# A hybrid decoder trunk: recurrence units of four head pairs by two chunks in place of two head pairs by four chunks

## The chip, the cores and the metric

The kernel runs on one core of a Trainium2 chip. The time is device microseconds of that core for one execution of the whole program; it is a median over runs. All matmuls run on TensorE (PE), which executes its instructions in the order in which they stand. VectorE (DVE), ScalarE (ACT) and GpSimd (POOL) work beside it, and the sync engine (SP) issues every DMA of the program, also in order.

## The reference, cut to what matters

A trunk of two layers over 1024 tokens with model width 1024 and 16 heads of 64. Layer 0 mixes time with the RWKV-7 recurrence, layer 1 attends to one shared set of keys and values; each is followed by an MLP. The recurrence is the part that the change touches:

```
S_t = S_{t-1} diag(w_t) + (S_{t-1} a_t) b_t^T + v_t k_t^T ;  y_t = S_t r_t     (per head, S is 64x64)
y   = groupnorm(y) * ln_w + ln_b + bonus
out = (y * (sigmoid(xg @ g1) @ g2)) @ wo
```

The decay is `w_t = exp(-exp(w_log))`, and `w_log` comes from a small product with `w2`. All arrays are float32.

## The kernel before, in words

Two heads share the 128 partitions and are called a pair; there are 8 pairs, and tokens are cut into chunks of 64. Inside a chunk the recurrence is turned into products, so that only the state (64x64 a head) goes from chunk to chunk. The work is cut into 16 units (`phase_wkv`). Each holds 8 pair-chunks: 2 pairs by 4 chunks, that is 256 tokens. `where(u)` gives the half of the sequence, the first pair and the tokens of unit `u`.

A unit has four parts, each a generator that yields at places where other work may be put in:

- `early` loads the unit's vectors (`ar`, `bk`), makes the decays (the product with `w2`) and inverts 16x16 blocks.
- `late` builds the chunk matrices (`sc`, `tt`, `bkt`) from them and loads the values `uv`.
- `chain` is the serial part. For each chunk it makes on TensorE the state product `pq<-st,ar`, with the output product `py<-ar,st` of the same state; VectorE adds (`xs`); then comes the solve product `pq<-xs,tt`, which ScalarE and VectorE copy to `uv`; then the state update `pq<-uv,bkt`, which VectorE adds to the scaled old state (`st`); then the second output product `py<-sc,uv`. Each is two matmuls a pair, one for each head.
- `gate` normalizes the unit's outputs and multiplies them by the gate: for each pair it loads `g2` into a buffer of one copy and makes two products with it (`pms<-ga,g` and `pms<-zt,g`).

Beside the chain the kernel runs `early` two units ahead, `late` one ahead, `gate` one behind, and the dense projections and the MLP of the first half (`beside`). After each yield of `chain`, `step` takes so many yields of the others as the table of numbers says (`PR`, `NG`, `NA` and so on). Chain instructions are recorded at high priority, and a scheduler sets the final order on each engine. Dense matmuls are of 128x512 columns (tiles `pj` and `pk`, lines 124 to 128), three for each weight block, since each operand is split in a high and a low part. Their weights pass through a ring of two raw buffers (`wraw`), ScalarE and GpSimd.

The fp32 matmuls of the chain use only a part of the array: 64 rows by 64 columns for those on `st` and `xs`, 128 rows by 64 columns for those on `uv`. The rows of the trace write this part ahead of the shape of the moving operand (`64*64`, `128*64`).

Of the kernel before, what the change touches and what calls it, by code (L numbers as in the profile page):

```python
# [15 lines left out]
F32 = mybir.dt.float32  # L16
# [3 lines left out]
ALU = mybir.AluOpType  # L20
# [55 lines left out]
class K:  # L76
# [168 lines left out]
    def run(self, stop=99):  # L245
        tc, nc, ap = self.tc, self.nc, self.ap
        V, S = nc.vector, nc.scalar
        with ExitStack() as es:
# [90 lines left out]
            self.smalls = [(pg, "pms", 1), (px, "pmt", 1)]  # L339
            x[1] = self.load_x(self.pool(es, "x1"), 1)  # L340
            e3 = es.enter_context(ExitStack())
# [3 lines left out]
            with ExitStack() as e2:  # L345
                self.mod_pool = self.pool(e2, "mp"), 2, D
                hs = self.gated(1, hp1)
                self.take(m0, self.ND[0])
                self.drain(self.proj([hs], wo, range(KT), self.residual(x, self.G[:, 0:8]), lead=2))
                m1 = self.mlp(x, 0, (1,), hp1, md)  # L350
                self.take(m1, 2)
                self.take(m0, self.ND[1])
                self.drain(m0)
                self.take(m1, 40)

                def mods():
# [11 lines left out]
                rs = self.rs = [xq.tile([128, HT], F32, name=f"rs{j}") for j in range(2)]  # L368
# [31 lines left out]

    N0 = 17
    NR = 4
    NMD = 4.5
    SG = 2
    EF = 1
    NG8 = 0.8
    UA = 7
# [8 lines left out]
    NS = 1.5  # L416
    NA = 2.2
    NW = (2, 2)
    NB = 5.4
    NC = 3  # L420
    NP = (3, 3, 3)
    PR = 2.2
    NG = 2
    ND = (20, 40)
# [16 lines left out]
    def phase_rwkv(self, es):  # L441
# [73 lines left out]
        if self.RP:  # L515
            with tc.high_priority():
                self.take(r, 1)
            self.take(r, 16)
        else:
            self.take(r, 17)  # L520
        v = self.stream(h, 0, 0, xj, ev, al)
# [146 lines left out]
    def phase_wkv(self, es, rest, done):  # L668
# [5 lines left out]
        H = (slice(0, 64), slice(64, 128))  # L674
        C = 8
        W = C * HD

        def where(u):

            j, g, q = u // 8, u % 8 // 2, u % 2  # L680
            return j, 2 * g, slice(j * HT + q * 256, j * HT + (q + 1) * 256)

        two = lambda a: a.rearrange("p (q t) -> p q t", q=2)
        pair = lambda d, p, ts: d[p:p + 2, :, ts].rearrange("q p t -> p q t")
        wa, pool = self.pool(es, "wkva", 2), {}
# [4 lines left out]
        def erl(n, shape, bufs=2):  # L690
            return wa.tile(shape, F32, name=n, tag=n, bufs=bufs)
# [24 lines left out]
        def early(u, w):  # L716

            j, p, ts = where(u)
            w2 = erl("w2", [65, 2, 128], 1)
            nc.sync.dma_start(out=w2, in_=ap["w2"][p:p + 2].rearrange("q k n -> k q n"))  # L720
            ar = erl("ar", [128, 2, C, HD], 3)
            bk = erl("bk", [128, C, 2, HD])
            nc.sync.dma_start(out=two(ar[:, 0].rearrange("p c t -> p (c t)")), in_=pair(self.kkd, p, ts))
            for i, src in enumerate((self.bd, self.kpd)):
                for q in range(2):
                    nc.sync.dma_start(out=bk[:, q * 4:(q + 1) * 4, i], in_=src[p + q, :, ts].rearrange("p (c t) -> p c t", t=HD))
            nc.sync.dma_start(out=two(ar[:, 1].rearrange("p c t -> p (c t)")), in_=pair(self.Rd, p, ts))

            Pi = erl("sg", [128, W], self.SG)
            ps = bank("pe")  # L730
            for q in range(2):
                PE.matmul(out=ps[:, q * 256:(q + 1) * 256], lhsT=w2[:, q], rhs=self.zt[0:65, ts], start=True, stop=True)
            yield
# [14 lines left out]
            kr = erl("sg", [128, W], self.SG)  # L748
            for i in range(2):
                q = slice(i * 4, i * 4 + 4)  # L750
                V.scalar_tensor_tensor(out=c3(kr)[:, q], in0=bk[:, q, 1], scalar=self.col("rk", p + i), in1=ar[:, 1, q], op0=ALU.mult, op1=ALU.mult)
# [21 lines left out]
        def late(u, w):  # L773
# [11 lines left out]
            uv = lng("uv", [128, C, 2, HD])  # L785
            for q in range(2):
                nc.sync.dma_start(out=uv[64:128, q * 4:(q + 1) * 4], in_=self.Vd[ts, (p + q) * 128:(p + q + 1) * 128].rearrange("(c s) (e d) -> s c e d", s=64, d=HD))

# [57 lines left out]
        def chain(u, w):  # L846
# [3 lines left out]
            yp = bank("py")  # L850
            old = self.sv[:, p:p + 2]
            begin, end = ts.start == 0, ts.stop == T
            of = lambda a: a.rearrange("p (q c) d -> p q c d", q=2)
            pc, xk = pc.rearrange("p (q c) -> p q c", q=2), of(xk)
            us = [of(uv[0:64, :, e]) for e in range(2)]

            def small(n, bufs=2):
                return lng(n, [128, 2, HD], bufs)

            def scaled(st, c):  # L860
                sp = small("sp")
                G.tensor_tensor(out=sp, in0=st, in1=pc[:, :, c:c + 1].broadcast_to([128, 2, HD]), op=ALU.mult)
                return sp

            def state():
                return bank("pq")[:, 0:128].rearrange("p (q d) -> p q d", q=2)

# [7 lines left out]
            sp = None if begin else scaled(old, 0)  # L875
            for c in range(4):
                first, last = begin and c == 0, end and c == 3
                ys = [yp[:, (q * 4 + c) * HD:(q * 4 + c + 1) * HD] for q in range(2)]
                xs = xk[:, :, c]
                if not first:  # L880
                    ps = state()
                    for q in range(2):
                        ins = both(ps[:, q], ar[:, 0, q * 4 + c], st[:, q], True, True)
                    for q in range(2):
                        both(ys[q], st[:, q], ar[:, 1, q * 4 + c], c + q == 0, False)
# [5 lines left out]
                for q in range(2):  # L891
                    ins = both(ps[:, q], tt[:, q * 4 + c], xs[:, q], True, True)
                S.copy(out=us[0][:, :, c], in_=ps[H[0]])
                yield ins, V.tensor_copy(out=us[1][:, :, c], in_=ps[H[1]])
                ins2 = None
                if not last:
                    ps = state()
                    st = small("st", 3) if c < 3 else old
                    for q in range(2):
# [6 lines left out]
                    if c < 3:  # L906
                        sp = scaled(st, c + 1)
                for q in range(2):
# [8 lines left out]
        def gate(u, w):  # L917

            j, p, ts = where(u)
            y, bv, rs = w["y"], self.t(), self.t()  # L920
            ga = lng("ga", [128, 256], 1)
            nc.sync.dma_start(out=ga, in_=self.gad[:, ts])
# [7 lines left out]
            ps = self.small()  # L930
            for q in range(2):
                c = slice(q * 256, (q + 1) * 256)
                g2 = lng("g2", [128, 2, 128], 1)
# [531 lines left out]
```

## Time and profile before

| what | value |
|---|---|
| median of 3 runs | 3394.16 us (3393.62 to 3395.95) |
| the profiled execution's own time | 3400.13 us |
| its span, first to last instruction | 3398.3 us |
| mean granted TensorE clock | 0.967 of full speed |
| chain of recurrences, first to last | about 332 to 1306 us |

All durations below are of the one profiled execution; its own time is 5.97 us above the median of the runs. TensorE is the busiest engine by far. The recurrence's stretch is the part of the span in which its small matmuls and the dense ones share TensorE.

### The profile page before, as it was taken

To read this page: it belongs to the slowest core of one execution; us is meant where nothing else is said; L and a number is where in the kernel's file an instruction comes from. 1 tells how busy PE (TensorE), PEld (TensorE's weight loads), DVE (VectorE), ACT (ScalarE), POOL (GpSimd) and SP (SyncE) were. 2 spreads that over 40 slices of the span, in tenths; PEclk is the share of its full clock that TensorE was granted. 3 is DMA by queue.
4 is the path that set the end of the run, shared out by engine and by line. 5 is a ranking of instruction groups with operands and counts; after the bars stand their busy time and mean duration, and the time that the engine had idled before them with its cause. 6 is when DMAs were issued, how large, how long until landed. Compare 5 with 4: busy or idle time off the path is not lost. (4 is left out here: it accounts for less than half of the span.)

```text
span 3398.3 us, 50336 instructions
## 1 busy us (share of the span) xinstructions
PE 3219.0 (95%) x19108; PEld 2442.9 (72%) x19108; DVE 1947.4 (57%) x3239; ACT 1434.2 (42%) x2284; POOL 1367.2 (40%) x868
## 2 busy tenths in 40 slices
PE   4898999999999999899999999999999999999997
PEld 2456666666777777678887777777778888778886
DVE  7496765756556535366676433555576666454444
ACT  3642236533433223242233556667565554332223
POOL 3364432333333233454444432444433333554444
PEclk7898999999999999899999999999999999999999
DMA  7365344454333225335542233666644442232322
GB/s 276 97 233 154 94 126 135 125 144 148 91 99 105 82 76 186 118 127 176 175 161 87 85 131 119 202 207 179 175 134 137 143 134 100 87 112 93 99 97 83
DMA packets 294066, 452.90 MB, mean 133 GB/s; under 512 B 114721, under 2 KB 170433, under 8 KB 293825
## 3 DMA queue, kind: packets, MB, share of 16 engines
q1 hardware_dynamic: 293824, 449.68, 42.0%
q8 instruction: 152, 2.49, 0.3%
q14 instruction: 90, 0.73, 0.1%
HBM read 371.25 MB, written 78.32 MB: 132 GB/s over the span
## 5 line engine op out<-in xcount | busy, mean ns | idle before, releaser
L117 POOL TENSOR_TENSOR wl<-wraw,wh 128x1024 fp32r<-128x1024 f32 x385 | 953.1, 2477 | 1221.7 <-ACT wh L116 1139.6
L116 ACT CAST wh<-wraw 128x1024 fp32r<-128x1024 f32 x385 | 402.6, 1046 | 835.2 <-PE pk L126 358.0
L124 PE MATMUL pj<-hh,wh 128*128 128x512 f32 x1120 | 449.4, 409 | 7.7 <-DVE sq L1085 2.1
L128 PE MATMUL pj<-hh,wl 128*128 128x512 f32 x1120 | 444.7, 403 | 6.0 <-POOL wl L117 6.0
L126 PE MATMUL pj<-hl,wh 128*128 128x512 f32 x1120 | 443.1, 401 | 0.0
L1011 DVE SCALAR_TENSOR_TENSOR x<-pj,G,x 128x512 f32<-128x512 f32 x304 | 225.8, 747 | 167.4 <-PE pj L128 165.6
L128 PE MATMUL pk<-hh,wl 128*128 128x512 f32 x688 | 273.7, 404 | 11.2 <-POOL wl L117 11.2
L124 PE MATMUL pk<-hh,wh 128*128 128x512 f32 x688 | 271.2, 400 | 7.9 <-ACT wh L116 6.7
L126 PE MATMUL pk<-hl,wh 128*128 128x512 f32 x688 | 268.6, 397 | 0.0
L124 PEld LDWEIGHTS pj<-hh,wh 128*128 128x128 f32 x1120 | 210.9, 189 | 62.5 <-issue 4.6
L128 PEld LDWEIGHTS pj<-hh,wl 128*128 128x128 f32 x1120 | 210.9, 188 | 60.2 <-POOL wl L117 8.2
L124 PE MATMUL pj<-mh,wh 128*128 128x512 f32 x564 | 237.7, 422 | 8.3 <-DVE x L1011 4.9
L126 PEld LDWEIGHTS pj<-hl,wh 128*128 128x128 f32 x1120 | 211.2, 189 | 47.2 <-issue 2.4
L1011 DVE SCALAR_TENSOR_TENSOR x<-pk,G,x 128x512 f32<-128x512 f32 x240 | 177.1, 747 | 110.9 <-PE pk L128 110.3
L126 PE MATMUL pj<-ml,wh 128*128 128x512 f32 x564 | 225.3, 399 | 0.0
L128 PE MATMUL pj<-mh,wl 128*128 128x512 f32 x564 | 219.5, 400 | 2.3 <-POOL wl L117 2.3
L124 PE MATMUL pk<-mh,wh 128*128 128x512 f32 x460 | 182.3, 398 | 7.0 <-DVE mr L1041 5.4
L166 ACT CAST mh<-mr 128x512 fp32r<-128x512 f32 x128 | 79.5, 621 | 248.4 <-PE pj L128 112.0
L126 PE MATMUL pk<-ml,wh 128*128 128x512 f32 x460 | 181.5, 395 | 0.0
L182 DVE SCALAR_TENSOR_TENSOR modacc<-modw,cact,modacc 128x1024 f32<-128x1024 f32 x98 | 158.6, 1619 | 31.9 <-DMA modw<-in_modw_dram 25.2
L128 PE MATMUL pk<-mh,wl 128*128 128x512 f32 x460 | 166.5, 398 | 0.0
L128 PEld LDWEIGHTS pk<-hh,wl 128*128 128x128 f32 x688 | 131.2, 191 | 45.3 <-POOL wl L117 15.0
(334 smaller groups left out, 6500.2 us busy)
## 6 DMA issues: line engine op xcount, KB each, us to landing
wraw<-in_up_dram SPq DMA_DIRECT2D x128, 512.0 KB
wraw<-in_down_dram SPq DMA_DIRECT2D x128, 512.0 KB
modw<-in_modw_dram SPq DMA_DIRECT2D x96, 512.0 KB
wraw<-in_wqg_dram SPq DMA_DIRECT2D x32, 512.0 KB
wraw<-in_wk_dram SPq DMA_DIRECT2D x24, 512.0 KB
wraw<-in_wv_dram SPq DMA_DIRECT2D x24, 512.0 KB
x<-in_xT_dram SPq DMA_DIRECT2D x32, 256.0 KB
wraw<-in_wr_dram SPq DMA_DIRECT2D x16, 512.0 KB
```

The lines of the kernel that those rows point to most:

```text
L116: nc.scalar.copy(out=wh, in_=raw)
L117: self.weng.tensor_tensor(out=wl, in0=raw, in1=wh.bitcast(F32), op=ALU.subtract)
L124: mm(out=p, lhsT=wh, rhs=hh[k], start=first, stop=False)
L126: mm(out=p, lhsT=wh, rhs=hl[k], start=False, stop=False)
L128: mm(out=p, lhsT=wl, rhs=hh[k], start=False, stop=last)
L166: self.nc.scalar.copy(out=out_h, in_=src)
L182: nc.vector.scalar_tensor_tensor(out=acc, in0=w, scalar=ck, in1=acc, op0=ALU.mult, op1=ALU.add)
L1011: self.nc.vector.scalar_tensor_tensor(out=x[j][m], in0=ps, scalar=gain[:, m:m + 1], in1=x[j][m], op0=ALU.mult, op1=ALU.add)
```

## The change

A unit now holds 4 pairs by 2 chunks (128 tokens). There are still 16 units of 8 pair-chunks, but a state is carried through 32 steps in place of 64, each with twice the pairs. The numbers of the table that count per chain step are doubled. Vectors are loaded in pieces of 128 tokens, and the products with `w2` and `g2` are made in twice as many pieces of half the columns; each unit's gate loads `g2` four times in place of two. Two edges are added: the second output products stand behind the state update of their step, and the next state product stands behind these outputs. Two small buffers change place (`x2` lies in `x1`, `rs` in the pool of the second half), and `st` has two buffers in place of three.

```diff
-    N0 = 17
+    N0 = 33
...
-    NA = 2.2
+    NA = 4.4
...
-    PR = 2.2
-    NG = 2
+    PR = 4.6
+    NG = 4
...
+        Q, N = 4, 2
...
-            j, g, q = u // 8, u % 8 // 2, u % 2
-            return j, 2 * g, slice(j * HT + q * 256, j * HT + (q + 1) * 256)
+            j, g, q = u // 8, u % 8 // 4, u % 4
+            return j, Q * g, slice(j * HT + q * 128, j * HT + (q + 1) * 128)
...
-                for q in range(2):
-                    nc.sync.dma_start(out=bk[:, q * 4:(q + 1) * 4, i], in_=src[p + q, :, ts].rearrange("p (c t) -> p c t", t=HD))
+                for q in range(Q):
+                    nc.sync.dma_start(out=bk[:, q * N:(q + 1) * N, i], in_=src[p + q, :, ts].rearrange("p (c t) -> p c t", t=HD))
...
-            for q in range(2):
-                PE.matmul(out=ps[:, q * 256:(q + 1) * 256], lhsT=w2[:, q], rhs=self.zt[0:65, ts], start=True, stop=True)
+            for q in range(Q):
+                PE.matmul(out=ps[:, q * 128:(q + 1) * 128], lhsT=w2[:, q], rhs=self.zt[0:65, ts], start=True, stop=True)
...
-            x2 = lng("x2", [128, C, 32], 1)
+            x2 = x1[:, :, 0:32]
...
-            for c in range(4):
-                first, last = begin and c == 0, end and c == 3
+            ins = None
+            for c in range(N):
+                first, last = begin and c == 0, end and c == N - 1
...
-                    for q in range(2):
-                        ins = both(ps[:, q], ar[:, 0, q * 4 + c], st[:, q], True, True)
+                    with ExitStack() as ea:
+                        if ins is not None:
+                            ea.enter_context(tc.issue_after(ins.ins))
+                        for q in range(Q):
+                            ins = both(ps[:, q], ar[:, 0, q * N + c], st[:, q], True, True)
...
-                            PE.matmul(out=ps[H[e], q], lhsT=bkt[:, q * 4 + c, e], rhs=uv[:, q * 4 + c, e], start=True, stop=True)
+                            ins = PE.matmul(out=ps[H[e], q], lhsT=bkt[:, q * N + c, e], rhs=uv[:, q * N + c, e], start=True, stop=True)
...
-                for q in range(2):
-                    for e in range(2):
-                        ins = PE.matmul(out=ys[q][H[e]], lhsT=uv[:, q * 4 + c, e], rhs=sc[:, q * 4 + c, e, 1], start=first and q == 0, stop=c + q == 4)
+                with tc.issue_after(ins.ins):
+                    for q in range(Q):
+                        for e in range(2):
+                            ins = PE.matmul(out=ys[q][H[e]], lhsT=uv[:, q * N + c, e], rhs=sc[:, q * N + c, e, 1], start=first and q == 0, stop=c == N - 1 and q == Q - 1)
...
-            ga = lng("ga", [128, 256], 1)
+            ga = lng("ga", [128, 128], 1)
...
-            for q in range(2):
-                c = slice(q * 256, (q + 1) * 256)
+            for q in range(Q):
+                c = slice(q * 128, (q + 1) * 128)
```

Where the instructions stand, first on TensorE in the middle of the recurrence. Before, from the gate products of one unit through the second half of a step's state update (`pq_6117`, line 901) to the next state product (`pq_6202`, line 870):

```order
L938 MATMUL pms_5932<-ga_5902,g2_5965 128x256
L939 MATMUL pms_5932<-zt_123,g2_5965 128x256
L804 MATMUL pl_6105<-uv_6045,sc_6048 64x64 x7
L901 MATMUL pq_6117<-uv_5361,bkt_5690 64x64
L870 MATMUL py_5878<-ar_4644,st_6118 64x64
L901 MATMUL pq_6117<-uv_5361,bkt_5690 64x64
L870 MATMUL py_5878<-ar_4644,st_6118 64x64
L804 MATMUL pl_6105<-uv_6045,sc_6048 64x64 x9
L710 MATMUL pl_6144<-dn1_1910,lb_5243 64x64 x8
L599 MATMUL pms_6156<-cs_60,e0_6153 128x128
L870 MATMUL pq_6202<-st_6118,ar_4644 64x64 x4
L870 MATMUL py_5878<-ar_4644,st_6118 64x64 x2
```

Now, at the like place: the last pair's state update (`pq_5693`, now line 907), the output products (line 917), and the next state product (`pq_5780`, now line 872).

```order
L712 MATMUL pe_5375<-ar_5336,bk_5337 64x64 x10
L124 MATMUL pj_5659<-xh_5587,wh_5648 128x512
L126 MATMUL pj_5659<-xl_5588,wh_5648 128x512
L128 MATMUL pj_5659<-xh_5587,wl_5649 128x512
L806 MATMUL pl_5670<-uv_5487,sc_5492 64x64 x5
L907 MATMUL pq_5693<-uv_4927,bkt_5244 64x64 x2
L917 MATMUL py_5312<-sc_4932,uv_4927 64x64 x8
L872 MATMUL py_5312<-ar_4164,st_5694 64x64 x6
L624 MATMUL pms_5291<-e1_5288,cs_60 128x512
L806 MATMUL pl_5670<-uv_5487,sc_5492 64x64 x2
L872 MATMUL pq_5780<-st_5694,ar_4164 64x64 x8
L872 MATMUL py_5312<-ar_4164,st_5694 64x64 x2
```

Single matmuls of lines 901 and 870, which use different parts of the array, stood in turn; now eight outputs, six outputs and eight state products stand in rows of their own.

Second, on the DMA queue, around one unit's gate (`g2` in, the gate of the unit before) and the weights of the dense work (`wraw`). Before:

```order
L115 DMA wraw_5823<-in_wv_dram 128x1024
L720 DMA w2_5886<-in_w2_dram 65x2x128
L643 DMA kkd_92<-e1_5154 128x512
L934 DMA g2_5281<-in_g2_dram 128x128
L935 DMA g2_5281<-in_g2_dram 32x128
L115 DMA wraw_5829<-in_wv_dram 128x1024
L922 DMA ga_5902<-gad_110 128x256
```

Now, with the loads of `uv` and of the inverted blocks (`dn0`, `dT0`) for the next `late`:

```order
L941 DMA g2_4845<-in_g2_dram 128x128
L942 DMA g2_4845<-in_g2_dram 32x128
L115 DMA wraw_5653<-in_wv_dram 128x1024
L941 DMA g2_4939<-in_g2_dram 128x128
L942 DMA g2_4939<-in_g2_dram 32x128
L789 DMA uv_5487<-Vd_100 64x2x128 x2
L772 DMA T16d_109<-ti_4873 64x2x256
L789 DMA uv_5487<-Vd_100 64x2x128
L941 DMA g2_4991<-in_g2_dram 128x128
L942 DMA g2_4991<-in_g2_dram 32x128
L785 DMA dn0_2014<-T16d_109 16x8x16
L785 DMA dT0_2015<-T16d_109 16x8x16
```

A unit has four loads of `g2` now, and each needs the buffer that the products with the one before have read; loads that `late` needs stand between and behind them.

## Rows read from the trace of the kernel before

**Rows 1.** The page, part 1: span; busy us, share of the span, records.
```profile
span 3398.3 us, 50336 instructions
...
PE 3219.0 (95%) x19108; PEld 2442.9 (72%) x19108; DVE 1947.4 (57%) x3239; ACT 1434.2 (42%) x2284; POOL 1367.2 (40%) x868
```

**Rows 2.** Us; PE, PEld, DVE, ACT, POOL busy (records); granted clock, DMA share, GB/s.
```profile
332.00:1306.00 974.00, 949.53 (x8618) 664.76 (x8617) 571.08 (x1270) 361.14 (x563) 334.19 (x268) 0.98 0.38 112
```

**Rows 3.** Instructions on tile pq: count, ns min/median/max, first and last start.
```profile
L901 PE MATMUL pq<-uv,bkt x480: 219/222/369, 338.3 to 1288.9; 128*64 128x64 f32 x160
```

**Rows 4.** TensorE's waits from 332 to 1306 us: total us, times, longest.
```profile
PE pj L126 <- DVE xl L167: 8.0, 4, 4.5
PE pq L870 <- DVE st L905: 4.0, 2, 3.0
...
PE pq L901 <- DVE st L903: 0.3, 1, 0.3
```

**Rows 5.** TensorE in order of time: start us, us, line, tile, records.
```profile
504.21 0.40 PE L124 MATMUL pj<-xh,wh 128*128 128x512 f32 x1
504.44 0.39 PE L126 MATMUL pj<-xl,wh 128*128 128x512 f32 x1
504.76 0.33 PE L901 MATMUL pq<-uv,bkt 128*64 128x64 f32 x2
505.02 0.33 PE L870 MATMUL py<-ar,st 64*64 64x64 f32 x2
505.27 0.33 PE L901 MATMUL pq<-uv,bkt 128*64 128x64 f32 x2
505.53 0.32 PE L870 MATMUL py<-ar,st 64*64 64x64 f32 x2
505.79 0.49 PE L128 MATMUL pj<-xh,wl 128*128 128x512 f32 x1
```

**Rows 6.** TensorE in order of time, three other places.
```profile
431.11 0.34 PE L901 MATMUL pq<-uv,bkt 128*64 128x64 f32 x4
431.37 0.50 PE L128 MATMUL pj<-xh,wl 128*128 128x512 f32 x1
...
509.89 0.45 PE L870 MATMUL pq<-xs,tt 64*64 64x64 f32 x8
510.27 0.37 PE L710 MATMUL pl<-x,dT 32*32 32x32 f32 x10
...
518.38 0.45 PE L870 MATMUL pq<-st,ar 64*64 64x64 f32 x8
518.66 0.28 PE L870 MATMUL py<-ar,st 64*64 64x64 f32 x4
518.88 0.31 PE L710 MATMUL pl<-tt,x 32*32 32x32 f32 x8
```

**Rows 7.** TensorE in order of time: one pair's gate products.
```profile
395.35 0.70 PE L938 MATMUL pms<-ga,g 128*128 128x256 f32 x2
395.98 0.69 PE L939 MATMUL pms<-zt,g 32*128 32x256 f32 x2
396.60 0.68 PE L710 MATMUL pe<-ar,bk 64*64 64x64 f32 x16
```

**Rows 8.** The DMA queue's own waits, 332 to 1306 us: total us, times, longest.
```profile
SPq L115 <- POOL wl L117: 197.8, 38, 13.1
SPq L934 <- PE pms L939: 42.5, 17, 7.2
```

**Rows 9.** DMA issues: count, ns min/median/max on the queue, first and last start.
```profile
L934 SPq DMA_DIRECT2D g<-in_g_dram x32: 327/346/1533, 282.6 to 1313.5; - x32
...
L726 SPq DMA_DIRECT2D bk<-bd x32: 359/462/697, 161.8 to 1095.8; - x32
...
L787 SPq DMA_DIRECT2D uv<-Vd x32: 585/606/1942, 297.6 to 1160.8; - x32
```

More of the change, by code (lines that the diff above doesn't have):

```diff
@@ L339, in run @@
             self.smalls = [(pg, "pms", 1), (px, "pmt", 1)]
-            x[1] = self.load_x(self.pool(es, "x1"), 1)
+            xq1 = self.pool(es, "x1")
+            x[1] = self.load_x(xq1, 1)
             e3 = es.enter_context(ExitStack())
@@ L367, in run @@
                 self.take(m1, 100)
-                rs = self.rs = [xq.tile([128, HT], F32, name=f"rs{j}") for j in range(2)]
+                rs = self.rs = [xq1.tile([128, HT], F32, name=f"rs{j}") for j in range(2)]
                 self.rms(x[0], rs[0])
@@ L405 @@
     EF = 1
-    NG8 = 0.8
+    NG8 = 1.6
     UA = 7
@@ L416 @@
     NS = 1.5
-    NA = 2.2
+    NA = 4.4
     NW = (2, 2)
-    NB = 5.4
-    NC = 3
+    NB = 10.8
+    NC = 6
     NP = (3, 3, 3)
-    PR = 2.2
-    NG = 2
+    PR = 4.6
+    NG = 4
     ND = (20, 40)
@@ L519, in phase_rwkv @@
         else:
-            self.take(r, 17)
+            self.take(r, 33)
         v = self.stream(h, 0, 0, xj, ev, al)
@@ L675, in phase_wkv @@
         C = 8
+        Q, N = 4, 2
         W = C * HD
         def where(u):
-            j, g, q = u // 8, u % 8 // 2, u % 2
-            return j, 2 * g, slice(j * HT + q * 256, j * HT + (q + 1) * 256)
-        two = lambda a: a.rearrange("p (q t) -> p q t", q=2)
-        pair = lambda d, p, ts: d[p:p + 2, :, ts].rearrange("q p t -> p q t")
+            j, g, q = u // 8, u % 8 // 4, u % 4
+            return j, Q * g, slice(j * HT + q * 128, j * HT + (q + 1) * 128)
+        two = lambda a: a.rearrange("p (q t) -> p q t", q=Q)
+        pair = lambda d, p, ts: d[p:p + Q, :, ts].rearrange("q p t -> p q t")
         wa, pool = self.pool(es, "wkva", 2), {}
@@ L718, in early @@
             j, p, ts = where(u)
-            w2 = erl("w2", [65, 2, 128], 1)
-            nc.sync.dma_start(out=w2, in_=ap["w2"][p:p + 2].rearrange("q k n -> k q n"))
+            w2 = erl("w2", [65, Q, 128], 1)
+            nc.sync.dma_start(out=w2, in_=ap["w2"][p:p + Q].rearrange("q k n -> k q n"))
             ar = erl("ar", [128, 2, C, HD], 3)
@@ L748, in early @@
             kr = erl("sg", [128, W], self.SG)
-            for i in range(2):
-                q = slice(i * 4, i * 4 + 4)
+            for i in range(Q):
+                q = slice(i * N, i * N + N)
                 V.scalar_tensor_tensor(out=c3(kr)[:, q], in0=bk[:, q, 1], scalar=self.col("rk", p + i), in1=ar[:, 1, q], op0=ALU.mult, op1=ALU.mult)
@@ L785, in late @@
             uv = lng("uv", [128, C, 2, HD])
-            for q in range(2):
-                nc.sync.dma_start(out=uv[64:128, q * 4:(q + 1) * 4], in_=self.Vd[ts, (p + q) * 128:(p + q + 1) * 128].rearrange("(c s) (e d) -> s c e d", s=64, d=HD))
+            for q in range(Q):
+                nc.sync.dma_start(out=uv[64:128, q * N:(q + 1) * N], in_=self.Vd[ts, (p + q) * 128:(p + q + 1) * 128].rearrange("(c s) (e d) -> s c e d", s=64, d=HD))
             sc = lng("sc", [128, C, 2, 2, HD])
@@ L850, in chain @@
             yp = bank("py")
-            old = self.sv[:, p:p + 2]
+            old = self.sv[:, p:p + Q]
             begin, end = ts.start == 0, ts.stop == T
-            of = lambda a: a.rearrange("p (q c) d -> p q c d", q=2)
-            pc, xk = pc.rearrange("p (q c) -> p q c", q=2), of(xk)
+            of = lambda a: a.rearrange("p (q c) d -> p q c d", q=Q)
+            pc, xk = pc.rearrange("p (q c) -> p q c", q=Q), of(xk)
             us = [of(uv[0:64, :, e]) for e in range(2)]
             def small(n, bufs=2):
-                return lng(n, [128, 2, HD], bufs)
+                return lng(n, [128, Q, HD], bufs)
             def scaled(st, c):
                 sp = small("sp")
-                G.tensor_tensor(out=sp, in0=st, in1=pc[:, :, c:c + 1].broadcast_to([128, 2, HD]), op=ALU.mult)
+                G.tensor_tensor(out=sp, in0=st, in1=pc[:, :, c:c + 1].broadcast_to([128, Q, HD]), op=ALU.mult)
                 return sp
             def state():
-                return bank("pq")[:, 0:128].rearrange("p (q d) -> p q d", q=2)
+                return bank("pq")[:, 0:Q * HD].rearrange("p (q d) -> p q d", q=Q)
             def both(ps, lhs, rhs, start, stop):
@@ L875, in chain @@
             sp = None if begin else scaled(old, 0)
-            for c in range(4):
-                first, last = begin and c == 0, end and c == 3
-                ys = [yp[:, (q * 4 + c) * HD:(q * 4 + c + 1) * HD] for q in range(2)]
+            ins = None
+            for c in range(N):
+                first, last = begin and c == 0, end and c == N - 1
+                ys = [yp[:, (q * N + c) * HD:(q * N + c + 1) * HD] for q in range(Q)]
                 xs = xk[:, :, c]
@@ L881, in chain @@
                     ps = state()
[L882 to L885 removed]
+                    with ExitStack() as ea:
[4 more added lines that the diff above has]
+                    for q in range(Q):
+                        both(ys[q], st[:, q], ar[:, 1, q * N + c], c + q == 0, False)
                     x = small("xs")
@@ L890, in chain @@
                 ps = state()
-                for q in range(2):
-                    ins = both(ps[:, q], tt[:, q * 4 + c], xs[:, q], True, True)
+                for q in range(Q):
+                    ins = both(ps[:, q], tt[:, q * N + c], xs[:, q], True, True)
                 S.copy(out=us[0][:, :, c], in_=ps[H[0]])
@@ L897, in chain @@
                     ps = state()
-                    st = small("st", 3) if c < 3 else old
-                    for q in range(2):
+                    st = small("st", 2) if c < N - 1 else old
+                    for q in range(Q):
                         for e in range(2):
-                            PE.matmul(out=ps[H[e], q], lhsT=bkt[:, q * 4 + c, e], rhs=uv[:, q * 4 + c, e], start=True, stop=True)
+                            ins = PE.matmul(out=ps[H[e], q], lhsT=bkt[:, q * N + c, e], rhs=uv[:, q * N + c, e], start=True, stop=True)
                         if first:
@@ L905, in chain @@
                             ins2 = V.scalar_tensor_tensor(out=st[:, q], in0=ps[:, q], scalar=pc[:, q, c:c + 1], in1=sp[:, q], op0=ALU.mult, op1=ALU.add)
-                    if c < 3:
+                    if c < N - 1:
                         sp = scaled(st, c + 1)
-                for q in range(2):
-                    for e in range(2):
-                        ins = PE.matmul(out=ys[q][H[e]], lhsT=uv[:, q * 4 + c, e], rhs=sc[:, q * 4 + c, e, 1], start=first and q == 0, stop=c + q == 4)
+                with tc.issue_after(ins.ins):
+                    for q in range(Q):
+                        for e in range(2):
+                            ins = PE.matmul(out=ys[q][H[e]], lhsT=uv[:, q * N + c, e], rhs=sc[:, q * N + c, e, 1], start=first and q == 0, stop=c == N - 1 and q == Q - 1)
                 yield ins, ins2
@@ L930, in gate @@
             ps = self.small()
-            for q in range(2):
-                c = slice(q * 256, (q + 1) * 256)
+            for q in range(Q):
+                c = slice(q * 128, (q + 1) * 128)
                 g2 = lng("g2", [128, 2, 128], 1)
```

## The prediction, made before the changed kernel had run

> **What bounds the kernel now.** I read the page first: TensorE is busy for 95% of the span, with no other engine over 57% [rows 1]. Then the busy time by stretch: from 332 to 1306 us, where the recurrence runs, TensorE is busy for 949.53 of 974.00 us at a granted clock of 0.98, while VectorE has 571 [rows 2]. So the stretch has only 24.5 us of idle TensorE. The serial chain takes 64 steps in 974 us, 15.2 us a step, and other work fills what a step waits for. The list of waits says how well: the longest is on `xl` of a dense projection, 8.0 us, which is no part of the chain; waits of the chain's own matmuls go from 4.0 us down to 0.3 us in six entries and sum to 10.1 us [rows 4]. Halving the number of steps therefore can't pay by shorter latency: there are 10 us of it to be had at most. What the stretch costs is TensorE's own time, and this must be read from start to start, since busy times of pipelined matmuls overlap.
>
> In order of time the reader sees two prices. Where matmuls of lines 901 and 870 alternate, four matmuls take from 504.76 to 505.79, 1.03 us or 0.26 each [rows 5]. (In the trace each fp32 matmul of the chain leaves two records: line 901 has 480 [rows 3] and 240 matmuls in the order, so x2 is one matmul.) Where matmuls of one array shape stand together, four take 0.38 us (509.89 to 510.27) and six 0.50 us (518.38 to 518.88) [rows 6]. So a piece, by which I mean a stretch of matmuls of one array shape that nothing of another shape interrupts, costs about 0.14 us and 0.06 us for each matmul; one alone costs 0.26, and two for the two heads also 0.26 (431.11 to 431.37) [rows 6]. The dense matmul shows the same edge: 0.23 us to the next dense one (504.21 to 504.44), 0.32 us to a small one (504.44 to 504.76), that is 0.09 more [rows 5].
>
> **The change part by part.** The chain keeps its 1232 matmuls; only how they stand is new. I counted pieces that hold chain matmuls over the whole TensorE order. Before there are 439: 234 of one matmul, 21 of two, 1 of three, 65 of four, 28 of five, 80 of six, 7 of seven, 3 of eight. Now there are 213: 14 of one, 89 of two, 14 of six, 42 of eight, 41 of ten, 1 of fourteen, 10 of sixteen, 2 of eighteen. With 0.26 for one or two and 0.14 + 0.06 n above, before costs 60.8 + 5.5 + 0.3 + 24.7 + 12.3 + 40.0 + 3.9 + 1.9 = 149.4 us, and now 3.6 + 23.1 + 7.0 + 26.0 + 30.3 + 1.0 + 11.0 + 2.4 = 104.4 us. **That is -45 us**, the main term. Eight and more are extrapolated by the slope.
>
> Dense work is the same 9648 matmuls, but it is cut into 593 stretches in place of 645: 52 x 0.09 = **-4.7 us**. The preparation (`early`, `late`) is cut a little more: 34 pieces more, each at the 0.14 us of a piece, **+4.8 us** (bounds 34 x 0.09 = 3 and 34 x 0.20 = 7, a lone matmul less its slope).
>
> The gate's two products for one pair and 256 tokens take 1.25 us (395.35 to 396.60) [rows 7]. Now two pairs of 128 tokens make the same columns with four matmuls. Were the cost all columns, this would be free; were it all overhead, +1.25 us for each of 32. By the slope, 64 columns of fp32 for two heads side by side take 0.12 us, so 256 columns take 0.48 and 128 take 0.24 us: a product of 0.63 us becomes 0.39, two pairs 1.56 in place of 1.25, 32 x 0.31 = **+10 us**. The decay products are split likewise, 32 matmuls more at between nothing and the 0.15 us that was overhead above; they stand with their own kind: **+2 us**. The Trainium skill, TensorEngine Tiling (Array Packing), section Performance Considerations, gives about 60 cycles of overhead for each matmul; at 2.4 GHz the 96 added matmuls would by that cost an estimated 2.4 us in place of my 12, and the sum would be 10 us lower. That page speaks of a matmul among its like, while rows here pay a change of shape too, so I keep the rows.
>
> The doubled vector operations (`xs`, copies to `uv`) save VectorE, ScalarE and GpSimd instructions; these engines are at 34 to 59% of the stretch [rows 2], so this is worth nothing where TensorE is full. The two moved buffers and the third `st` are free as long as their readers are done, which the chain's order forces anyway. 16 projection steps (48 dense matmuls, 11 us) are demanded ahead of the recurrence in place of in it; the same TensorE time elsewhere, counted at nothing. If they found idle TensorE there they would gain up to 11 us; if the start were late instead, the same 11 would be lost.
>
> The waits: the new edges put eight outputs ahead of the next state product, which stands behind the VectorE updates anyway, and in the listing they are what TensorE does while VectorE updates `st`; behind the waiting matmul stand the other units' work and the dense work. Half the steps with more work between them should at least halve 10.1 us: **-5 us** (bounds: -10, all gone; and +10, each of 32 steps waiting 0.6 us).
>
> Sum: -45 - 4.7 + 4.8 + 10 + 2 - 5 = **-38 us**. The profiled execution took 3400.13 us, its span 3398.3; that gives 3362 us for its like. It lies 5.97 us above the median of the runs, so I forecast **3356 us** (1.1% faster). About 0.2%, 7 us, is what a measurement of this kernel can tell from no change.
>
> **The rivals.** *The chain becomes the bound.* Each step has twice the width, one bank `pq` and four state updates in a row on VectorE. If a step made TensorE wait 1.2 us more than now, 32 steps would give back the 38 us and the time would stay at 3394 us. For it speaks that every step still has three round trips to VectorE; against it, that there is 30 us of TensorE work for each step and that the other matmuls which the new order puts within a round trip, priced as above, come to 2.5 to 5 us at the median of each of the three.
>
> *The DMA queue becomes the bound, and the kernel is slower.* Each unit's four `g2` loads use one buffer, and the queue stands still until TensorE has made the gate product that reads it. Before, this held the queue for 42.5 us in 17 waits [rows 8]. Twice the loads make twice the waits, +42 us, and the change adds 160 issues: 64 for `g2`, 64 for `bk`, 32 for `uv`, at 0.35 to 0.61 us each [rows 9], some +75 us with the second `g2` load put near 0.4. Behind a waiting load stand weight loads and the loads that `late` needs. The queue's slack is what it waits for free weight buffers, 197.8 us [rows 8], against 117 us more: enough on the mean. If the loads bunch and TensorE paid for two thirds of the 117, 78 us, the sum would be +40 us: 3434 us; it decides at a third, 38 us, where the gain is gone. The Trainium skill, DMA: Bandwidth & Descriptors, section Bandwidth, says that transfers under 64 KB are descriptor-dominated and that DMAs should be batched, which speaks against this change: it halves `bk` and `uv` pieces. No row here shows a transfer's price by size in this stretch; the DMA engines' share is 0.38 [rows 2].
>
> *The overhead of a piece is hidden.* If TensorE's starts were held by something else than the change of shape, fewer pieces would give less: with half the main term, -15 us and 3379 us. Against it: 0.26 us repeats four times in a row without any wait [rows 5].
>
> **How the numbers follow.** Forecast (gain of 20 to 70 us): 0.68. Overhead half hidden, 3379 us: 0.10, faster still. Chain bound, 3394 us: 0.10, of which 0.07 within 0.2% and 0.03 faster. DMA queue: 0.12, of which 0.10 slower and 0.02 within 0.2%. So faster 0.81, within 0.2% 0.09, slower 0.10. Low end: all bounds the good way, -45 - 5 + 3 + 0 + 0 - 10 = -57, and the 2% of clock that the stretch doesn't get [rows 2], 19 us, half won back: 3328 us, taken at 3324 for the 11 us at the start in part. High end: the chain-bound case and the first few us of the slower one, 3398 us; this leaves out about 0.04 below and 0.09 above.
>
> **What would show it.** In the changed profile: the recurrence's stretch shorter by about 28 us of dense work that moves behind it (some 120 matmuls) and by about 38 us for good; x8 and longer runs of records where x2 alternated; rows from start to start of 0.62 us for eight; the gate's pair at near 0.78 us; the sum of TensorE's waits on `st`, `xs` and `uv` at or under 10 us; weights not waited for. It is wrong if TensorE's idle time in the stretch rises beyond 25 us, if its waits name DMA, `wh` or `wl`, or if a run of eight takes well over 0.7 us.

## The result, and the profile after

The changed kernel is slower: 3439.41 us, median of four runs (3435.31 to 3443.17), against 3395.05 us for the kernel before (3393.62 to 3407.53), a ratio of 1.011 with a 95% interval of 1.0092 to 1.0129. The forecast was 3356 us. The profiled execution took 3435.31 us.

The page, part 1, answers to [rows 1]: the span is 34.9 us longer, and yet TensorE's busy time is the same.

```profile
span 3433.2 us, 50825 instructions
...
PE 3217.2 (94%) x19300; PEld 2472.5 (72%) x19300; DVE 1984.3 (58%) x3273; ACT 1431.9 (42%) x2252; POOL 1353.1 (39%) x838
```

The busy time by stretch, over the recurrence (columns as in [rows 2]):

```profile
343.00:1306.00 963.00, 910.35 (x8650) 665.50 (x8650) 580.95 (x1277) 349.22 (x518) 307.52 (x229) 0.94 0.39 111
```

Here the reader is to see three things. The stretch begins 11 us later and ends where it ended. TensorE is busy for 39 us less, of which some 29 us (0.23 us each) are 123 dense matmuls that now stand outside the stretch, 8 ahead of it and 115 behind. And two losses are new: 52.6 us of idle TensorE in place of 24.5, and a granted clock of 0.94 in place of 0.98. The clock has two levels, 1.2 and 2.4 GHz; the clock's records put 122.9 us of the stretch at the lower one, against 47.8 us before.

To set these against each other I split the span of each kernel into idle time (gaps of more than 0.2 us between TensorE's records), half of the time at the low level outside the gaps (what that level adds), and the rest, which is the work at full clock. For the whole span, in us:

| kernel | span | idle | low level, half | work at full clock |
|---|---|---|---|---|
| before | 3398.3 | 161.3 | 86.4 | 3150.6 |
| changed | 3433.2 | 198.1 | 118.7 | 3116.5 |
| difference | +34.9 | +36.8 | +32.3 | -34.1 |

The terms of the prediction that are work, all but the waits, sum to -45 - 4.7 + 4.8 + 10 + 2 = -33 us. The work fell by 34 us. What failed is the rest of the sum. Two cautions on this table: the 15.9 us behind the last matmul are in no gap, and counted as one they make the last two differences +33.7 and -35.6; and each column is of one execution, so a few us in it mean little.

TensorE's waits from 343 to 1306 us (columns as in [rows 4]):

```profile
PE pe L712 <- DVE bk L744: 8.2, 2, 4.9
PE pms L945 <- DMA g<-in_g_dram: 4.9, 5, 1.7
PE pms L945 <- ACT t L935: 4.6, 2, 4.1
PE pms L637 <- ACT e L638: 3.5, 2, 2.7
PE pq L907 <- DVE uv L900: 3.3, 3, 1.5
PE pl L796 <- DVE sc L800: 2.9, 2, 2.4
PE pj L128 <- POOL wl L117: 2.9, 1, 2.9
PE pq L907 <- DVE sv L911: 2.8, 3, 2.0
```

Only two of these eight are the chain's. By what waits, the chain's matmuls went from 10.0 to 15.2 us, the preparation (`pe`, `pl`) from 1.8 to 14.6, the gate from 0 to 11.4, the projections' small products from 0.2 to 6.0; the dense matmuls fell from 11.4 to 4.5. The new waits are in the work that was to cover the chain.

How a wait and the clock hang together is seen best at one place, TensorE in order of time:

```profile
507.78 0.40 PE L128 MATMUL pj<-xh,wl 128*128 128x512 f32 x1
508.65 0.34 PE L907 MATMUL pq<-uv,bkt 128*64 128x64 f32 x4 [0.48 <-DVE uv L900]
513.93 1.97 PE L712 MATMUL pe<-ar,bk 64*64 64x64 f32 x32 [4.94 <-DVE bk L744]
515.84 0.79 PE L945 MATMUL pms<-ga,g 128*128 128x128 f32 x2
...
524.34 0.63 PE L124 MATMUL pj<-xh,wh 128*128 128x512 f32 x1
524.77 0.63 PE L126 MATMUL pj<-xl,wh 128*128 128x512 f32 x1
525.19 0.63 PE L128 MATMUL pj<-xh,wl 128*128 128x512 f32 x1
...
531.35 0.40 PE L128 MATMUL pj<-xh,wl 128*128 128x512 f32 x1
531.59 0.40 PE L124 MATMUL pj<-xh,wh 128*128 128x512 f32 x1
531.92 0.68 PE L872 MATMUL pq<-st,ar 64*64 64x64 f32 x16
532.43 0.28 PE L872 MATMUL py<-ar,st 64*64 64x64 f32 x4
532.65 0.50 PE L126 MATMUL pj<-xl,wh 128*128 128x512 f32 x1
```

A product of the preparation, `pe<-ar,bk`, waits 4.94 us for `bk`. From 510.8 to 531.3 us the granted clock is at the lower level: dense matmuls stand 0.43 us apart, in place of 0.23. The wait cost 4.94 us by itself, and the 17.4 us at the low level behind it another 8.7. The rows also show the forecast mechanism at work: eight state products side by side take 0.51 us (531.92 to 532.43), where I had put 0.62.

VectorE at that place shows why `bk` was late:

```profile
507.79 0.35 DVE L944 SCALAR_TENSOR_TENSOR y<-y,prm,t 128x128 f32<-128x128 f32 x1
508.17 0.43 DVE L900 COPY uv<-pq 64x256 f32<-64x256 f32 x1
508.52 2.41 DVE L943 SCALAR_TENSOR_TENSOR y<-y,prm,t 128x128 f32<-128x128 f32 x1
510.85 2.42 DVE L944 SCALAR_TENSOR_TENSOR y<-y,prm,t 128x128 f32<-128x128 f32 x1
513.20 0.67 DVE L744 SCALAR_TENSOR_TENSOR bk<-bk,sg 128x512 f32<-128x512 f32 x1
```

Two gate operations that take 0.35 us elsewhere took 2.4 us each, ahead of `bk` in VectorE's order; the last section shows what held them.

The DMA queue's own waits answer to [rows 8]:

```profile
SPq L115 <- POOL wl L117: 131.2, 35, 10.9
SPq L941 <- PE pms L946: 69.0, 29, 5.8
```

The wait for the one `g2` buffer rose from 42.5 us in 17 waits to 69.0 in 29, and the queue's slack fell from 197.8 to 131.2 us.

### The profile page after: what moved, and what is told of

It reads as the page before. It is cut to its first block, busy times and chain, and to the rows that moved or that the text cites. A ratio compares the mean times of both kernels' runs of the same rounds, so it can differ in the third digit from the quotient of the medians.

```text
span 3433.2 us, 50825 instructions
## 1 busy us (share of the span) xinstructions
PE 3217.2 (94%) x19300; PEld 2472.5 (72%) x19300; DVE 1984.3 (58%) x3273; ACT 1431.9 (42%) x2252; POOL 1353.1 (39%) x838
## 5 line engine op out<-in xcount | busy, mean ns | idle before, releaser
L124 PE MATMUL pj<-hh,wh 128*128 128x512 f32 (+1 forms) x1128 | 454.7, 411 | 9.1 <-ACT wh L116 2.6
L128 PE MATMUL pj<-hh,wl 128*128 128x512 f32 (+1 forms) x1128 | 449.0, 404 | 8.6 <-POOL wl L117 8.6
L126 PE MATMUL pj<-hl,wh 128*128 128x512 f32 (+1 forms) x1128 | 447.3, 402 | 0.0
L128 PE MATMUL pk<-hh,wl 128*128 128x512 f32 x680 | 269.8, 403 | 10.3 <-POOL wl L117 10.3
L124 PEld LDWEIGHTS pj<-hh,wh 128*128 128x128 f32 (+1 forms) x1128 | 213.4, 189 | 64.2 <-issue 5.0
L128 PEld LDWEIGHTS pj<-hh,wl 128*128 128x128 f32 (+1 forms) x1128 | 213.4, 189 | 63.6 <-POOL wl L117 11.5
L126 PEld LDWEIGHTS pj<-hl,wh 128*128 128x128 f32 (+1 forms) x1128 | 213.7, 190 | 50.7 <-issue 3.9
L182 DVE SCALAR_TENSOR_TENSOR modacc<-modw,cact,modacc 128x1024 f32<-128x1024 f32 x98 | 160.5, 1638 | 31.5 <-DMA modw<-in_modw_dram 25.0
```

What stands on the lines that cost most here:

```text
L124: mm(out=p, lhsT=wh, rhs=hh[k], start=first, stop=False)
L126: mm(out=p, lhsT=wh, rhs=hl[k], start=False, stop=False)
L128: mm(out=p, lhsT=wl, rhs=hh[k], start=False, stop=last)
L182: nc.vector.scalar_tensor_tensor(out=acc, in0=w, scalar=ck, in1=acc, op0=ALU.mult, op1=ALU.add)
```

## The experiments

The theories were these. **A:** the saved work is real, and more waits of TensorE, each with a stretch of low clock behind it, ate it; the waits come from the unit's shape, through the queue of `g2` loads and the bunched preparation. **B:** the two edges cost, since they force what TensorE does next. **C:** the clock fell because small matmuls of a part of the array run long without a dense one, whatever the waits. Each run is compared with runs of the kernel before on the same chip, so the ratio is the figure to read; "idle" and "low" are of the recurrence's stretch (before: 23.4 and 47.8 us; changed: 51.8 and 122.9).

| run | median us | ratio, 95% interval | work, whole span | idle | low |
|---|---|---|---|---|---|
| e1 shape without edges | 3434.04 | 1.0099 (1.0084 to 1.0114) | -25 | 45.8 | 122.9 |
| e2 edges in the old shape | 3390.87 | 0.9970 (0.9951 to 0.9989) | -39 | 42.1 | 61.4 |
| e3 changed, two `g2` buffers | 3417.42 | 1.0050 (1.0035 to 1.0065) | -39 | 44.0 | 126.3 |
| e4 changed, slower preparation | 3425.13 | 1.0071 (1.0056 to 1.0086) | -29 | 47.9 | 116.1 |
| e5 e3 and e4 together | 3407.31 | 1.0020 (1.0007 to 1.0032) | -39 | 35.7 | 102.4 |
| e6 changed, 96 dense added | 3462.78 | 1.0180 (1.0162 to 1.0198) | -3 | 47.2 | 126.3 |
| e7 e2 with two `g2` buffers | 3385.47 | 0.9957 (0.9942 to 0.9972) | -37 | 38.4 | 71.7 |
| e8 changed, one `g2` load a unit | 3417.55 | 1.0050 (1.0033 to 1.0066) | -41 | 40.9 | 109.2 |
| e9 before, longer chain step | 3464.62 | 1.0194 (1.0171 to 1.0217) | -2 | 55.0 | 109.2 |
| e10 e7 with slower preparation | 3399.88 | 0.9996 (0.9980 to 1.0012) | -31 | 40.8 | 75.1 |
| e11 e5 with more dense demanded | 3409.49 | 1.0031 (1.0019 to 1.0043) | -34 | 45.5 | 85.3 |

Medians of the kernel before: 3399.19 us beside e1 to e4, 3402.05 beside e5 to e8, 3400.95 beside e9 to e11. The work is of the profiled execution, against 3150.6 us; that execution can lie some us from the median (e5's took 3398.35 us, the shortest of its 12).

**Shape or edges (e1, e2).**

```diff
# e1, on the changed kernel
-                        if ins is not None:
-                            ea.enter_context(tc.issue_after(ins.ins))
...
-                with tc.issue_after(ins.ins):
# e2: the same lines put into the kernel before
```

> The changed kernel (3439 us) with its two added edges taken out, so the unit shape alone. Theory 1 (fewer pieces save TensorE time, but the new unit shape makes TensorE wait and its clock fall): slower than the changed kernel by the 12 us that its chain pieces cost more (291 pieces, 117 us by the price of a piece, against 213 and 104), about 3450 us, with idle TensorE in the recurrence's stretch near 50 us and a clock near 0.94 as in the changed kernel. Rival (the edges make TensorE wait): at or under 3395 us, with idle time near 25 us.

> The kernel before (3395 us) with the two edges alone, units of two pairs by four chunks. Its chain stands in 311 pieces in place of 439, 118 us by the price of a piece in place of 149. Theory 1: faster than before by 15 to 35 us, 3360 to 3380 us. Rival (the edges make TensorE wait): 3395 us or slower, with more than 10 us of waits on the chain's tiles.

Without the edges the new shape stays slow (1.0099), with as much time at the low level; it was to be 12 us slower than the changed kernel and is not: in its profiled execution 9 us more of work stand beside 4 us less of idle time, and by its median it is no slower. The edges alone, in the old shape, make the kernel 0.3% faster, where 15 to 35 us were expected. So theory B falls as the cause of the loss: that is the shape's. The single `g2` buffer is in e1 too, and there the gate's waits are only 3.9 us while the chain's are 17.0, so which group waits depends on the order. The work says more. By the prediction's count of pieces, 439 of before become 311 with the edges alone (-31 us by its prices), 291 with the shape alone (-32) and 213 with both (-45). Measured, the edges alone save 39 us of work and both together 34: it looks as if what the shape joins further is given back by its split products and its cut preparation, but the kernels with the new shape and the edges scatter from -29 to -41 us. Of e2's 39 us, 8 arrived; its span has 27 us more idle time, and the chain's own waits went from 10.0 to 20.0 us, the sign that the rival of e2 had named. So the edges cost waits too, but the low level rose by 14 us only. The stretch of e2 (columns as in [rows 2]):

```profile
334.00:1290.00 956.00, 911.99 (x8593) 642.14 (x8592) 574.20 (x1267) 359.58 (x560) 328.44 (x266) 0.97 0.38 113
```

**The queue behind `g2` (e3, e8).**

```diff
# e3
-                g2 = lng("g2", [128, 2, 128], 1)
+                g2 = lng("g2", [128, 2, 128], 2)
# e8, around the load and its two DMAs
+                if q == 0:
```

(`xs` has one buffer in e3, to make room.)

> The changed kernel with two buffers for g2 (and one for xs, to make room), so that a load of g2 waits for the product two before it. If the DMA queue standing still at g2 is what costs: most of the loss is back, 3390 to 3410 us, and the queue's wait at g2 falls from 69 us to under 20. Theory 1 (waits of many kinds, of which g2 is one): 3425 to 3439 us.

> The changed kernel with one load of g2 for each unit in place of four; the products of all four pairs use the first pair's g2, so three quarters of the gate's weights are left out. It takes 96 of 128 DMA issues and all waits of the queue for the g2 buffer but one a unit. Theory A, the number of issues on the queue is a cost beside the wait for the buffer: clearly under the run with two buffers (3417 us), at 3405 us or less. Theory B, only the wait for the buffer cost: 3410 to 3420 us, like two buffers. Waits of TensorE in the gate under 5 us in both.

Both end at a ratio of 1.005. A second buffer gave 22 us back by the medians (21 by the ratios), half of the loss. That is between the two expectations. TensorE's waits in the gate fell from 11.4 to 4.2 us and the preparation's from 14.6 to 5.4, while the chain's rose from 15.2 to 21.7; `xs` with one buffer was not tried alone. Taking away three quarters of the loads in place of the second buffer gave the same, to about 5 us, though the queue had more slack. Its own waits in e8 (columns as in [rows 8]; line 929 loads `ga`, the gate's other operand, and waits at the head of a unit's gate) are

```profile
SPq L115 <- POOL wl L117: 179.9, 34, 10.3
SPq L929 <- PE pms L946: 27.0, 6, 7.5
```

So it is the wait for the buffer that cost, and not the number of issues. In e3 the queue still waits long for `g2`, where under 20 us were expected, and the gate's matmuls hardly notice:

```profile
SPq L941 <- PE pms L946: 56.6, 23, 9.0
```

**Bunched preparation (e4, e5).**

```diff
-    PR = 4.6
-    NG = 4
+    PR = 3.4
+    NG = 1.6
```

> The changed kernel with 3.4 in place of 4.6 yields of preparation and 1.6 in place of 4 yields of gate after each chain yield, so that they spread over the whole unit. If preparation and gate are recorded too densely for their own latencies, so that TensorE reaches their matmuls before the data: idle time in the stretch falls from 53 us to 30 or less and the clock rises, 3395 to 3415 us. If not: within 10 us of 3439 us.

> The changed kernel with two g2 buffers (xs has one) and with the preparation and the gate spread over more chain yields (PR 3.4, NG 1.6), both at once. Theory A, two separate losses (the queue behind g2, and bunched preparation): the gains of 22 and 14 us add, 3439 to about 3403 us, ratio 1.003, idle TensorE in the recurrence's stretch 40 us or less. Theory B, both runs removed the same waits: no more than the 22 us of the better one, 3415 to 3420 us, ratio 1.005 to 1.007. Either way the low clock stays above 100 us in the stretch unless it follows the idle time.

(The change had raised PR from 2.2 to 4.6, a little more than doubling it.) Spread over more of a unit's chain yields, the preparation gave 14 us back, less than expected, and the stretch's idle time fell by 4 us only, not to 30. With two buffers as well, 31 of the 34 us that the two gave apart by the ratios are there: two separate causes, as theory A had it. The stretch of e5 is now (columns as in [rows 2])

```profile
343.00:1278.00 935.00, 898.49 (x8633) 653.22 (x8633) 588.49 (x1275) 345.18 (x516) 308.06 (x229) 0.95 0.40 114
```

TensorE is idle for 36.5 us of it (35.7 in gaps over 0.2 us), at a clock of 0.95. Its work is 39 us less than before, and idle time (+21 us over the span) and low clock (+16) take nearly all of it in this execution, the shortest; by all its runs the ratio is 1.002.

**Does a wait bring the clock down (e9), or a lack of dense matmuls (e6, e11)?**

```diff
# e9, kernel before, behind the xs add
+                    for i in range(4):
+                        ins2 = V.tensor_copy(out=x, in_=x)
# e6, changed kernel, ahead of a group of small matmuls
+            PE.matmul(out=ps, lhsT=carry[:, 0:128].bitcast(F32R), rhs=carry.bitcast(F32R), start=True, stop=True)
# e11, on e5
-    NA = 4.4
-    NC = 6
+    NA = 5.0
+    NC = 6.8
```

> The kernel before with four more copies of xs onto itself on VectorE behind each xs add: some 0.6 to 0.8 us more on the chain's path for each of 64 steps, and no TensorE work more. Theory A, a wait of TensorE costs more than its length, since a fall of the clock follows it (in the kernel before 48 us at low clock stand beside 23 us of idle time in the recurrence's stretch): idle TensorE rises by 10 to 30 us, time at low clock by twice that, and the time by about twice the idle time, 3415 to 3455 us. Theory B, the clock goes by the shape of the unit and not by waits: the low clock stays under 60 us and the time rises by the idle time alone. Theory C, other work fills the longer step: within 0.2%, 3388 to 3402 us.

> The changed kernel with 96 more matmuls of the dense kind (128x512 columns, full array, on a constant), each put ahead of one of the preparation's groups of small matmuls, into a bank that the group overwrites; the result is not changed. At 0.23 to 0.32 us it is 22 to 31 us of work more. Theory A, the granted clock falls where small matmuls of a part of the array run long without a dense one: time at low clock in the recurrence's stretch falls from 123 to 70 us or less, which gives back 25 us or more, and the time is 3425 to 3445 us. Theory B, the clock falls because TensorE stands idle: the low clock stays at 110 us or more and the time is 3460 to 3475 us.

> The changed kernel with two g2 buffers and slower preparation, and with more dense work demanded for each chain yield of the first ten units (NA 5.0 in place of 4.4, NC 6.8 in place of 6), so that the recurrence's stretch holds as many dense matmuls as before the change or more. Theory A, the clock stays low for longer in the changed shape because its stretch holds fewer dense matmuls: low clock in the stretch falls from 102 to 80 us or less, and the time from 3407 to 3390 to 3400 us. Theory B, the low clock goes by the waits and by how the small matmuls stand: low clock of 95 us or more, the same dense work only moves from the tail into the stretch, 3402 to 3412 us.

e9 adds nothing to TensorE's work and changes little in its order (427 pieces in place of 439); only waits are made. Its stretch (columns as in [rows 2]):

```profile
332.00:1365.00 1033.00, 976.21 (x8608) 684.25 (x8608) 654.95 (x1512) 361.25 (x561) 326.59 (x266) 0.95 0.36 105
```

TensorE's longest waits in it (columns as in [rows 4]), both the chain's:

```profile
PE pq L870 <- DVE xs L889: 20.4, 13, 5.4
PE pq L903 <- DVE st L907: 8.2, 4, 4.7
```

Over the span, idle time rose by 36.0 us, the low level's half by 27.5, and the work moved by -2: the span is 61.4 us longer, 1.7 times the waits. These are nearly the changed kernel's two losses, in the old shape and with the old work. **That added waits cost well over their length is shown for this run.** It is no fixed price: in e2, the same shape, 27.0 us of idle time came with 3.7 us through the clock. My expectation had put the ratio at 2 and the end of the range at 3455.

In e6 the added matmuls cost what they should (work 31.5 us above the changed kernel's, 0.33 us each), and the low level stayed at 126.3 us. So theory C, in the form that one dense matmul ahead of each small group would help, falls. e11 was to raise the dense count and hardly did (1724 to 1733 in the stretch): the low level fell to 85.3 us, the idle time rose to 45.5, and the time stayed. It tells nothing on C, and it shows again that low level and idle time need not move together.

**A version that beats both (e7, e10).** e7 is e2 with two `g2` buffers and one of `xs`; e10 spreads the preparation besides.

```diff
# e10, on e7
-    PR = 2.2
-    NG = 2
+    PR = 1.7
+    NG = 0.8
```

> The kernel before with the two edges and with two g2 buffers (xs has one). Theory A, the queue's wait for g2 costs in any shape: some 5 to 10 us under the edges alone, 3381 to 3386 us. Theory B, the old shape loads g2 half as often and its queue has slack: no gain over the edges alone, 3388 to 3395 us; one xs buffer in place of two can cost up to 5 us.

> The kernel before with the two edges, two g2 buffers, and the preparation and the gate spread over more chain yields (PR 1.7 in place of 2.2, NG 0.8 in place of 2). Theory A, the bunched preparation makes waits in this shape too, as in the changed one where the same step gave 14 and 12 us: 3370 to 3379 us, idle TensorE in the recurrence's stretch under 32 us, low clock under 60 us. Theory B, the old shape's waits are of its chain and its dense work: no gain over the edges with two buffers, 3382 to 3390 us.

e7 is the fastest kernel of the study, 0.4% under the kernel before. It ran beside other kernels than e2, and the intervals of the two overlap, so what the second buffer adds in the old shape is not settled. Slower preparation, which helped the changed shape, cost 13 us here by the ratios, which neither theory had: waits of the chain went from 17.6 to 24.6 us, though all idle time in the stretch rose by 2.4 us only.

## Why the prediction was wrong

**The main term held, as a sum.** Fewer and longer pieces, dearer gate and decay products and a more cut preparation were put at -33 us of work; -34 was measured. That it fits to 1 us is luck, since the other kernels with this shape and these edges give -29 to -41, and e2's 39 us for a priced 31 suggests errors that cancel. One part of it was low: the gate's pair of products for 128 tokens takes 0.83 us where the clock is full (two products of 128 columns from 453.03 to the next matmul at 453.86), not 0.78. The 120 dense matmuls that were to move behind the stretch were 115.

**The step that failed is "The waits": -5 us, with bounds of -10 and +10.** Measured, 36.8 us more of idle time over the span. I took the chain's own 10.1 us as all that could change, and asked what the new order puts within the chain's round trips. But TensorE runs in order, and each group of the preparation and of the gate has waits of its own, for VectorE, ScalarE or a load. With half the chain yields, the same groups were demanded twice as fast at each, and a load of `g2` could start only when the products with the last had been made. These matmuls were cover before, with 1.8 us of waits in all; now they waited 26 us themselves. The bound of "+0.6 us a step" was looked for in the wrong matmuls. That the edges cost no wait, since VectorE's updates come first anyway, did not hold either: in e2 they alone doubled the chain's waits. Two of the prediction's three signs of being wrong came: idle time beyond 25 us, and waits that name a DMA and `wl`; a run of eight stayed short.

**A step that was missing: the clock.** The sum took 0.98 as given, and its low end even counted on winning half of the other 2%. It cost 32 us more, nearly as much as the waits themselves. The price stood in [rows 2]: 24.5 us of idle time stood beside a clock 2% under full in 974 us. The Trainium skill, TensorE: Matmul & The Clock Gate, section "A second HAM failure mode: psum-queue depth-cycling", tells of a kernel whose engine idled briefly and often between groups of matmuls: its clock swung between the two levels, and throughput suffered although the median matmul was that of full speed. The traces agree: 15 stretches at the low level in place of 7, and in e9 27.5 us beside 36.0 us of waits.

**The queue rival was half right.** It was to cost 78 us if two thirds of its new waits reached TensorE; 22 us did (e3), by its mechanism, the single `g2` buffer, and the 96 issues that e8 took away had cost nothing that could be measured. That its 3434 us lie near the measured 3439 is luck. The mean slack, by which I had set its chance low, was no cover for loads that come in bunches: 131.2 us of slack were left while TensorE waited for `g2`. **The chain did not become the bound:** its own waits rose by 5 us, against 38 that this rival needed. **The piece overhead was not hidden:** e2 got 39 us of work from order alone.

**The start.** The 48 dense matmuls demanded ahead of the recurrence were counted at nothing, with 11 us lost if the start were late. It was 10.3 us late: 8.3 us of work, 3.7 of idle time, less the clock's part. But the 48 are not there: in TensorE's order 576 dense matmuls stand ahead of the first state product, against 570 before. The records that are new there besides are of small products: 28 of `pj<-t,lw` for 16 of `pk<-t,lw`, the split decay products, 8 more of `pms<-cs,e`. How much of it is only moved was not measured, and an earlier start wasn't tried.

**What stays open.** At like idle time the changed shape has more time at the low level: e5 102.4 us beside 35.7, e7 71.7 beside 38.4. What sets how long it lasts is not shown. Dense matmuls in the stretch are a rival to the waits: they go with the low level at least as well as idle time does, at 1.89 a us before (47.8 us low), 1.92 in e2 (61.4) and 1.91 in e7 (71.7), but 1.84 in e5 (102.4), 1.80 in e9 (109.2) and 1.78 in the changed kernel (122.9). Three of the changed kernel's 15 low stretches (from 684.9, 838.5 and 947.7 us) have no wait over 1 us near ahead of them. At the place shown above the level rose while dense matmuls ran again, behind some 5 us of small ones, and the changed shape's pieces of small ones are longer; but e6 did not bear that out for single dense matmuls, and no run here made longer runs of them. Nor is the rest of e5's waits traced to one cause, and no run gave `st` its third buffer or the two moved buffers their old places back.

## What to carry to other kernels

Where an engine is 95% busy, split a change into work, waits and clock, and forecast each: a saving of work of 1% is lost to waits of 0.6% if each costs 1.7 times its length, as in e9. When the unit of a software pipeline is reshaped, look at the covering work for its own waits (single buffers, groups demanded in bunches), and not at the bottleneck chain alone. Reordering within the old shape is the cheaper trial: here two ordering edges alone gave all of the saved work and a kernel that was 0.3% faster.

## What the runs showed of the hardware

**The price of short waits.** In the changed kernel, all 8 waits of TensorE over 2 us in the stretch, and 5 of 11 between 1 and 2 us, had the low level at or soon behind them; before, 2 of 2 and 3 of 7. In the stretches of all 13 kernels it was so for 73 of the 76 waits over 2 us. The low level lasted 8.2 us on the mean (15 times) and 6.8 (7 times), and up to 20.5 us; in e9 once 30.7 us, behind a wait of 4.74 us, while few dense matmuls ran.

**VectorE beside GpSimd.** The two gate operations of 2.41 and 2.42 us above lie beside GpSimd's `wl`, in order of time on GpSimd:

```profile
508.44 4.69 POOL L117 TENSOR_TENSOR wl<-wraw,wh 128x1024 fp32r<-128x1024 f32 x2 [1.31 <-ACT wh L116]
```

Two `wl` in 4.69 us: each VectorE operation is as long as one of them, and the second ends at 513.27 us, 0.14 us behind the second `wl`. The whole traces show the same: all 12 of the changed kernel's 128 gate operations that took over 0.5 us end 0.14 to 0.16 us behind the end of a GpSimd operation, and the 103 beside which GpSimd ran nothing took 0.33 to 0.35 us. Such an operation stood until GpSimd's was done. The kernel before has 64 of them, twice as wide, of which 5 were held so (their ends 0.28 us behind); the time lost rose from 6 to 17 us of VectorE. It is not by itself the loss, for in e4 over 30 took as long and e4 is faster than the changed kernel. The Trainium skill, GPSIMD Engine Reference, section "1. Specifications", says that GpSimd's SBUF interfaces are shared with VectorE, with contention where a VectorE instruction has two SBUF inputs, as lines 943 and 944 have. The traces agree; no run here took `wl` off GpSimd to show what that would give back.
